# Storing 16 of the last 24 output tiles in smaller pieces: RMSNorm and matmul on one core

## The chip, the cores and the metric

One core of a Trainium2 chip runs the kernel. The metric is the device time of one execution in microseconds (us), the median of several runs; lower is better. Profiles show a span, from the first to the last instruction, which is some 1.5 to 2 us shorter than the device time of the same kernel. All times inside a run are counted from the start of its span.

Loads and stores are carried out by 16 DMA engines that move data between the chip's memory and the core. A store is *issued* when it is put on the queue; each engine then moves its share and counts up the store's completion semaphore, and the time of that is called the *landing* on this engine. The *backlog* of an engine is what it was given earlier and has not moved yet.

## The reference

```python
batch, seq, dim, out_dim = 16, 1024, 512, 768        # all float32
rms = np.sqrt(np.mean(x ** 2, axis=-1, keepdims=True) + eps)
x_norm = x / rms * gamma
return np.matmul(x_norm, weight).astype(np.float32)
```

The 16,384 rows are cut into 128 tiles of 128 rows. A tile of output is 128 x 768 float32, 384 KB, or 3 KB on each of 128 partitions. In all 35.13 MB are read and 50.33 MB written.

## The kernel before

TensorE transposes the rows and multiplies in bfloat16; ScalarE and VectorE take turns in scaling a finished tile out of PSUM, the memory that TensorE writes to, into an output buffer `ot` that holds eight tiles; SyncE issues every load and store on one queue (but for the 2 KB of gamma). `stretches` says which tiles are stored together, and a store is issued when the last tile of its stretch is written:

```python
NT, XG, OG = 128, 16, 8
opening = [1, 1, 1, 1, 2, 2]
last = NT // OG - 1                                   # 15: tiles 120 to 127
o_first, o_size = stretches(OG, {0: opening, 1: [4, 4], last - 1: [4, 4], last: [2, 2, 1, 1, 1, 1]})
...
outp = ctx.enter_context(tc.tile_pool(name="out", bufs=3))
...
def store(i):
    first, n = o_first[i], o_size[i]
    if i == first + n - 1:
        nc.sync.dma_start(out=rows(out, first, n), in_=held(o_tiles, OG, first, n))
...
def finish_tile(i, acc, engine):                      # for each tile, in order
    scale(engine, out_tile(i), acc[:, :O], rstd_of[i])
    store(i)
```

Groups that the table doesn't name go by eight. The very last tile is stored in two parts (columns 0 to 511, then the rest). A packet of a store is one partition's run: 24 KB for eight tiles, 12 for four, 6 for two, 3 for one.

Of the kernel before, what the change touches and what calls it, by code (L numbers as in the profile page):

```python
# [18 lines left out]
def kernel(  # L19
# [18 lines left out]
    XG, OG = 16, 8  # L38
# [7 lines left out]
    def stretches(group, parts):  # L46
        first, size, i = {}, {}, 0
        for g in range(NT // group):
            for n in parts.get(g, [group]):
                for t in range(i, i + n):  # L50
                    first[t], size[t] = i, n
                i += n
        return first, size

    opening = [1, 1, 1, 1, 2, 2]
    last = NT // OG - 1
    x_first, x_size = stretches(XG, {0: opening + [4, 4], 1: [4, 4, 8], 2: [8, 8]})
    o_first, o_size = stretches(OG, {0: opening, 1: [4, 4], last - 1: [4, 4], last: [2, 2, 1, 1, 1, 1]})

    def rows(ap, i, n):  # L60
        if i < XG:
# [287 lines left out]
```

## Time and profile before

| | before |
|---|---|
| median of 3 runs, us | 210.98 (210.57 to 211.02) |
| span of the profiled run, us | 209.0 |
| TensorE busy | 96% |
| DMA data queue, share of 16 engines | 97.0% |
| last matmul ends, us | 203.1 |
| last store lands, us | 207.98 |

The last matmul ends 4.8 us before the last byte has landed. The lines of the page, the stretches at the end and the waits stand in the prediction below, with how they are read.

### The profile page before, as it was taken

How to read it: one execution, taken by the hardware profiler on the slowest of the kernel's cores; microseconds unless marked ns; L12 is line 12 of the kernel's file. 1: busy time of each engine (PE TensorE's matmuls, PEld its weight loads, DVE VectorE, ACT ScalarE, POOL GpSimd, SP SyncE). 2: the span in 40 equal slices, each digit the busy share in tenths (PEclk: the TensorE clock that was granted, in tenths of full speed). 3: DMA queues.
4: the chain of work that ended last, by engine and by line, in shares of the span. 5: the costliest groups of instructions: out<-in, count | busy, mean ns of one | idle time of the engine just before them, and what ended most of it. 6: DMA issues, size and time to landing. Idle time of an engine off the chain costs nothing.

```text
span 209.0 us, 3534 instructions
## 1 busy us (share of the span) xinstructions
PE 201.6 (96%) x1298; PEld 137.9 (66%) x1298; DVE 109.0 (52%) x173; ACT 149.6 (72%) x359; POOL 67.0 (32%) x73
## 2 busy tenths in 40 slices
PE   7999999999999999999999999999999999999980
PEld 2466777666766776667766776667667766677640
DVE  0465654654565465456545644654564465456550
ACT  2689987787778778777877777787777778777640
POOL 1357532306331073213623062310633045230000
PEclk9999999999999999999999999999999999999999
DMA  6999999999999999999999999999999999899994
GB/s 231 392 430 422 408 395 436 424 414 439 431 458 411 412 442 425 447 411 437 428 448 419 423 423 442 433 433 417 428 442 447 405 441 414 381 386 386 383 374 182
DMA packets 7077, 85.69 MB, mean 410 GB/s; under 512 B 786, under 2 KB 916, under 8 KB 3476
## 3 DMA queue, kind: packets, MB, share of 16 engines
q1 hardware_dynamic: 7056, 85.46, 97.0%
q8 instruction: 10, 0.16, 0.3%
q14 instruction: 7, 0.06, 0.1%
q10 hardware_dynamic: 4, 0.00, 0.0%
HBM read 35.13 MB, written 50.33 MB: 409 GB/s over the span
## 4 chain that ended last, share of the span: by engine, by line
PE 91%; ACT 3%; DMA 2%; POOL 1%; DVE 1%; issue 0%; SPq 0%
PE ops L168 77%; PE tp L133 13%; DMA xt<-in_x_dram 2%; ACT jk L98 1%; ACT ot L150 1%; POOL xb L94 1%; ACT rms L102 0%; DVE xT L140 0%; PE ops L227 0%; DVE ot L152 0%; SPq L206 0%; DVE rstd L104 0%
## 5 line engine op out<-in xcount | busy, mean ns | idle before, releaser
L168 PE MATMUL ops<-w_bf,xT 128*128 128x256 bf16 (+1 forms) x1024 | 194.2, 326 | 0.3 <-DVE xT L140 0.3
L168 PEld LDWEIGHTS <-xT 128*128 128x128 bf16 x1024 | 100.0, 98 | 56.4 <-DVE xT L140 1.4
L94 POOL CAST xb<-xt 128x1024 bf16<-128x1024 f32 (+1 forms) x67 | 66.3, 1002 | 118.9 <-PE tp L133 72.9
L150 ACT ACTIVATE ot<-ops,rstd 128x768 f32<-128x768 f32 (+1 forms) x65 | 58.1, 894 | 47.2 <-PE ops L168 47.2
L140 DVE COPY xT<-tp 128x1024 bf16<-128x1024 bf16 (+1 forms) x67 | 44.7, 667 | 83.3 <-PE tp L133 83.0
L98 ACT ACTIVATE jk<-xt 128x512 bf16<-128x512 f32 x128 | 78.7, 619 | 0.7 <-DMA xt<-in_x_dram 0.7
L133 PE MATMUL tp<-ident_f,xb 128*128 128x128 f32 x256 | 68.9, 273 | 0.1
L152 DVE TENSOR_SCALAR ot<-ops,rstd 128x768 f32<-128x768 f32 (+1 forms) x65 | 64.5, 993 | 2.9 <-PE ops L168 2.9
L133 PEld LDWEIGHTS tp<-ident_f,xb 128*128 128x128 f32 x256 | 35.9, 141 | 3.8 <-POOL xb L94 0.7
L98 ACT ACTIVATION_READ_ACCUMULATOR jk<-xt 128x1 f32 x128 | 24.4, 191 | 0.0
L102 ACT ACTIVATE rms<-ssq,eps_sb 128x4 f32<-128x4 f32 (+3 forms) x35 | 10.4, 297 | 1.1
L104 DVE RECIPROCAL rstd<-rms 128x4 f32<-128x4 f32 (+3 forms) x35 | 5.9, 167 | 3.3 <-ACT rms L102 3.3
L227 PE MATMUL ops<-warm 128*128 128x512 bf16 x16 | 6.4, 561 | 1.2 <-DVE eps_sb L220 1.2
L227 PEld LDWEIGHTS <-warm 128*128 128x128 bf16 x16 | 1.9, 131 | 3.9 <-issue 2.5
L150 ACT ACTIVATE w_bf<-w_f,g_sb 128x768 bf16<-128x768 f32 x2 | 1.9, 936 | 3.6 <-DMA w_f<-in_weight_dram 3.6
L201 ACT ACT_TABLE_LOAD x1 | 1.3, 1283 | 1.3 <-PEq L330 1.3
L152 DVE TENSOR_SCALAR w_bf<-w_f,g_sb 128x512 bf16<-128x512 f32 (+2 forms) x3 | 1.4, 485 | 1.1 <-DMA w_f<-in_weight_dram 1.0
L241 DVE COPY g_sb<-tp 128x4 f32<-128x4 f32 x1 | 0.2, 162 | 3.1 <-PE tp L239 3.1
L239 PEld LDWEIGHTS tp<-ident_f,g_row 2*128 2x128 f32 x2 | 0.3, 200 | 0.8 <-issue 0.8
L218 DVE MEMSET warm<- 128x256 uint32 x1 | 0.3, 272 | 0.9 <-PEq L330 0.9
L239 PE MATMUL tp<-ident_f,g_row 2*128 2x2 f32 x2 | 0.4, 264 | 0.0
masks.py:199 POOL TENSOR_SCALAR_AFFINE_SELECT ident_f<-ident_f 128x128 f32<-128x128 f32 x1 | 0.3, 292 | 0.1
(6 smaller groups left out, 0.7 us busy)
## 6 DMA issues: line engine op xcount, KB each, us to landing
out_dram<-ot SPq DMA_DIRECT2D x12, 3072.0 KB, 16.3
xt<-in_x_dram SPq DMA_DIRECT2D x5, 4096.0 KB, 23.0
xt<-in_x_dram SPq DMA_DIRECT2D x3, 2048.0 KB, 19.4
out_dram<-ot SPq DMA_DIRECT2D x4, 1536.0 KB, 11.6
xt<-in_x_dram SPq DMA_DIRECT2D x4, 1024.0 KB, 13.2
out_dram<-ot SPq DMA_DIRECT2D x4, 768.0 KB, 10.4
out_dram<-ot SPq DMA_DIRECT2D x7, 384.0 KB, 11.2
w_f<-in_weight_dram SPq DMA_DIRECT2D x2, 768.0 KB, 5.9
```

The lines of the kernel that those rows point to most:

```text
L94: engine.tensor_copy(out=xb_tiles[i // 2][:, i % 2:i % 2 + n, :], in_=held(x_tiles, XG, i, n))
L98: nc.scalar.activation(out=jk, in_=held(x_tiles, XG, i)[:, 0, :], func=AF.Square, accum_out=ssq)
L102: nc.scalar.activation(out=rms[:, :n], in_=ssq[:, :n], func=AF.Sqrt, scale=1.0 / D, bias=eps_sb)
L104: nc.vector.reciprocal(out=rstd[:, :n], in_=rms[:, :n])
L133: nc.tensor.transpose(out=tp_tiles[j][:, t, h, :], in_=words[:, lo:lo + P], identity=ident_f)
L140: nc.vector.tensor_copy(out=dst[:, t:t + n, :], in_=src[:, t:t + n, :])
L150: nc.scalar.mul(out=dst, in_=src, mul=r)
L152: nc.vector.tensor_single_scalar(out=dst, in_=src, scalar=r, op=mybir.AluOpType.mult)
L168: nc.tensor.matmul(out=acc[:, lo:hi], lhsT=xT_tiles[i // 2][:, i % 2, k // 2, :, k % 2], rhs=w_bf[:, k, lo:hi], start=(k == 0), stop=(k == ...
L201: nc.scalar.preload_act_table(AF.Sqrt)
L227: nc.tensor.matmul(out=spare[:, :WIDE], lhsT=warm[:, :P], rhs=warm, start=True, stop=True)
L239: nc.tensor.transpose(out=gp[:, c, :], in_=g_row[:, :, c], identity=ident_f[:2, :2])
```

## The change

The intent: store tiles 104 to 119 in smaller pieces, so that DMA engines which have run dry get something earlier and less is left at the end.

```diff
-    o_first, o_size = stretches(OG, {0: opening, 1: [4, 4], last - 1: [4, 4], last: [2, 2, 1, 1, 1, 1]})
+    o_first, o_size = stretches(OG, {0: opening, 1: [4, 4], last - 2: [4, 4], last - 1: [2, 2, 2, 2],
+                                 last: [2, 2, 1, 1, 1, 1]})
```

Tiles 104 to 111 go by 4 + 4 instead of 8, tiles 112 to 119 by 2 + 2 + 2 + 2 instead of 4 + 4. The edit is a line longer, so line numbers in later profiles are one higher (165 becomes 166).

## The prediction

> **What bounds the kernel now.** I read the page of the kernel before first: busy time, the forty slices, then the chain that ended last.
>
> ```profile
> PE 201.6 (96%) x1298; PEld 137.9 (66%) x1298; DVE 109.0 (52%) x173; ACT 149.6 (72%) x359; POOL 67.0 (32%) x73
> ...
> DMA  6999999999999999999999999999999999899994
> GB/s 231 392 430 422 408 395 436 424 414 439 431 458 411 412 442 425 447 411 437 428 448 419 423 423 442 433 433 417 428 442 447 405 441 414 381 386 386 383 374 182
> ...
> PE 91%; ACT 3%; DMA 2%; POOL 1%; DVE 1%; issue 0%; SPq 0%
> ```
>
> The reader is to see two nearly full resources. TensorE is busy 96% of 209.0 us and 91% of the chain, but the sixteen DMA engines are at nine tenths too (the page puts the data queue at 97.0% of them). The one 8 in the DMA row is in slice 35, from about 178 to 183 us. The change touches only stores after 174 us, so it can act only through the DMA queue and the end of the run. I therefore cut the last 39 us by hand, with the windows view: columns are the stretch, its length, busy us (and instructions) of PE, PEld, DVE, ACT, POOL, the granted clock, the DMA share and GB/s.
>
> ```profile
> 170.00:179.00 9.00, 9.00 (x61) 6.28 (x60) 4.94 (x7) 6.55 (x17) 5.09 (x5) 1.00 1.01 429
> 179.00:182.00 3.00, 3.00 (x21) 2.13 (x20) 1.70 (x3) 2.38 (x7) 1.04 (x1) 1.00 0.75 320
> 182.00:192.00 10.00, 10.00 (x67) 7.00 (x66) 5.46 (x8) 7.55 (x20) 2.08 (x2) 1.00 0.95 406
> 192.00:194.00 2.00, 2.00 (x16) 1.39 (x15) 1.17 (x3) 1.38 (x4) 0.00 (x0) 1.00 0.59 246
> 194.00:199.00 5.00, 5.00 (x35) 3.36 (x33) 3.15 (x5) 2.74 (x7) 0.00 (x0) 1.00 1.00 415
> 199.00:200.50 1.50, 1.50 (x11) 0.95 (x10) 0.16 (x1) 0.90 (x1) 0.00 (x0) 1.00 0.71 291
> 200.50:206.00 5.50, 2.64 (x17) 1.37 (x14) 1.99 (x3) 1.37 (x2) 0.00 (x0) 1.00 1.00 395
> 206.00:208.00 2.00, 0.00 (x0) 0.00 (x0) 0.00 (x0) 0.00 (x0) 0.00 (x0) 0.99 0.14 51
> ```
>
> TensorE never pauses up to 203 us. The DMA engines as a group starve three times, near 180, 193 and 199.5 us, because no store is ready; that is what the change goes after. After 200.5 they are full again, until 206, and then something small drags on to 208. The waits of the DMA-issuing queue after 160 us name the end:
>
> ```profile
> SPq L165 <- DVE ot L152: 41.6, 8, 11.8
> SPq L344 <- DMA out_dram<-ot: 3.5, 1, 3.5
> ```
>
> The first line says that stores wait for results, not for one another. The second is the end of the program, which waits 3.5 us for a store: the last vector result is written at 203.66 us (in the timeline, started 203.18, 0.48 long), the last store is issued at 203.88 and lands at 207.98, and the span ends 1.0 us later. So the end is set by when the last store lands.
>
> **Which engine drags.** The average over engines hides it. A store's completion semaphore gets sixteen updates in the trace, one per DMA engine, so I read each store by engine:
>
> | store (issued at, us) | first 12 landed by | the four late ones |
> |---|---|---|
> | tiles 96-103 (168.87) | 181.85 | 183.62, 184.56, 184.93, 185.14 |
> | tiles 104-111 (181.00) | 189.66 | 190.88, 191.85, 192.37, 192.52 |
> | tiles 112-115 (187.07) | 193.32 | 194.54, 196.02, 196.34, 196.94 |
> | tiles 116-119 (193.15) | 198.22 | 198.24, 199.66, 200.14, 200.60 |
> | tiles 120-121 (196.19) | 200.08 | 200.12, 201.52, 202.09, 202.44 |
> | tiles 122-123 (199.22) | 202.46 | 202.48, 203.32, 204.03, 204.24 |
> | second part of 127 (203.88) | 206.43 | 206.48, 207.12, 207.81, 207.98 |
>
> Twelve or thirteen engines catch up with the stores at each pause and finish by 206.48. Three never do: from 185 us to the end they go from one store to the next, and end 0.6 to 1.5 us after the rest. Instruction fetches explain much of the lag: the trace has ten of 16 KB, some 0.95 us each on one engine, the last three at 156.96, 176.06 and 194.66 us. The bytes that those three engines have left set the end, not the time at which a store is ready.
>
> **What the Trainium skill says.** "DMA: Bandwidth & Descriptors", section "Queues, rings and completion order": on each engine descriptors are consumed in ring order. The trace agrees: on the late engines, landings of successive stores follow one another by exactly the service time, 1.80 to 1.95 us for 6 KB pieces. Its section "Why a DMA increments its semaphore by 16 and not by 1" says that a DMA runs on up to 16 engines that finish independently and the semaphore counts them; the spread of 183.62 to 185.14 after 181.85 is that. Section "Rules for kernel authors" wants at least 1 MiB per DMA for bandwidth. Here a queue with a backlog hardly shows it: packets of 24, 12 and 6 KB took 921, 468 and 239 ns after 170 us, 26.7, 26.3 and 25.7 bytes per ns. Section "Anatomy of one DMA" puts a fixed 2 us on a DMA of the GpSimd path; back to back these stores from SyncE show no such gap, and the last landing is 0.33 us after the last packet's end.
>
> **The change part by part.**
> 1. Tiles 104 to 111: one store of eight (3072 KB) becomes two of four. The first is issued when tile 107 is out, four tiles earlier: 181.00 - 2 x 3.04 = 174.9 us (a pair of tiles takes 3.04 us in the timeline). It removes most of the pause at 180 us: 3 us at a share of 0.75, so 0.75 us of group time.
> 2. Tiles 112 to 119: two stores of four become four of two, issued at about 184.0, 187.1, 190.1 and 193.15. The pause at 193 (2 us at 0.59, 0.8 us) is broken up and moved: with less backlog, the twelve engines now pause before each later store.
> 3. On the twelve engines the end stays: they already wait at 199.7 to 200.1 for the store of 199.22, and from there the remaining stores and their issue times are untouched. End still 206.4.
> 4. On the three late engines nothing is filled, because nothing was empty. Their bytes are the same in smaller pieces. One engine's share, from landing to landing on the late engines: eight tiles 7.28 us, four tiles 3.66, two tiles 1.84. Tiles 104-111: 2 x 3.66 - 7.28 = +0.04. Tiles 112-119: 4 x 1.84 - 2 x 3.66 = +0.04. Sum +0.08; three more completion writes at 9 ns add 0.03. Together +0.1 us on the path that sets the end.
> 5. SyncE issues three more DMAs at 0.33 us: 1 us, beside 41.6 us in which it waits for results, so hidden. Computation, its buffers and their releases are the same: the buffers of tiles 104 to 119 are not reused after.
>
> So the time goes from 210.98 by +0.1 to **211.1 us**.
>
> **Rivals.** (a) *The pauses are filled and the end comes forward.* For it: the group loses about 2 us in the three pauses (0.75 + 0.8 + 0.4). Were the whole backlog gone, the late engines would end with the others: 207.98 - 206.48 = 1.5 us, giving 209.5, a gain of 0.7%. Against: the three engines had no pauses. The bound on any gain is thus under 2% even if I am wrong. (b) *Small stores cost more than the landings show*, say a fixed 0.3 us each on a backlogged engine: three more stores would add 0.9 us, 211.9. Against: the 3 KB stores near the end follow each other at 0.92 to 0.95 us on the late engines for eight packets of 123 ns, no bubble. (c) *TensorE waits for a buffer that a store holds*: the output pool rotates by three groups, tile 112 needs the store of tiles 88-95 (landed 178.06) and tile 120 that of 96-103 (185.14 against its first write at 193.4). Neither is touched, so nothing. (d) *The late engines are others, or less late, in runs without the profiler*: an instruction fetch that falls elsewhere moves the end by up to its 0.95 us, in both kernels. It widens the range, without a direction.
>
> **Range and chances.** The runs before lie from 210.57 to 211.02. From 211.1 I go down to 210.4, half of (a) or a lucky fetch, and up to 211.7, most of (b). Over 2% is 4.2 us either way: no rival reaches half of it. Faster 0.01, within 2% 0.98, slower 0.01.
>
> **What would show it.** Right: pauses at 180 and 193 us smaller or broken up in the slices, the first twelve landings of the last store still near 206.4, three late engines still going without a pause, last landing 207.9 to 208.2, matmuls ending at the same 203.2 us. Wrong: late landings that close up on the twelve, with a last landing near 206.5 (rival a); successive landings of two-tile stores on late engines over 2 us apart (rival b); a new wait of ACT or DVE for a DMA (rival c).

## The result, and the profile after

The changed kernel took 210.95 us (210.82 to 211.13, 6 runs) beside 210.87 us of the kernel before (210.57 to 211.02, 6 runs). The ratio is 1.0007, with a 95% interval from 0.9994 to 1.0020: the same. Ratios here are the mean time of one kernel's fast runs over the mean of the other's fast runs of the same rounds, so they are not quite the ratio of the medians.

First the page of the changed kernel, the lines that answer to those shown of before.

```profile
PE 199.9 (96%) x1273; PEld 137.7 (66%) x1298; DVE 109.0 (52%) x173; ACT 149.6 (71%) x359; POOL 67.0 (32%) x73
...
DMA  6999999999999999999999999999999999999884
GB/s 219 387 429 423 409 405 431 430 409 448 424 451 416 412 437 430 434 437 421 427 448 424 416 437 432 434 429 409 441 426 434 434 429 418 420 417 395 345 336 171
```

The 8 in slice 35 is a 9 now: the pause near 180 us is gone. But two 8s have come in slices 38 and 39. (25 matmul records fewer are a gap in the record, not in the program: weight loads are 1298 in both.) The windows of the changed kernel, with the columns and, from 179 us on, the stretches that the prediction used, say the same in more detail: the last two columns are the DMA share and GB/s.

```profile
179.00:182.00 3.00, 2.95 (x21) 2.10 (x21) 1.70 (x3) 2.38 (x7) 1.04 (x1) 1.00 0.92 393
182.00:192.00 10.00, 9.95 (x67) 6.98 (x67) 5.39 (x8) 7.55 (x20) 2.08 (x2) 1.00 0.99 419
192.00:194.00 2.00, 2.00 (x15) 1.40 (x14) 1.24 (x3) 1.38 (x4) 0.00 (x0) 1.00 0.84 347
194.00:199.00 5.00, 4.95 (x33) 3.39 (x33) 3.07 (x5) 2.81 (x7) 0.00 (x0) 1.00 0.84 344
199.00:200.50 1.50, 1.50 (x11) 0.93 (x10) 0.23 (x1) 0.90 (x1) 0.00 (x0) 1.00 0.49 201
200.50:206.00 5.50, 2.71 (x18) 1.42 (x15) 1.98 (x3) 1.37 (x2) 0.00 (x0) 1.00 0.99 394
206.00:208.00 2.00, 0.00 (x0) 0.00 (x0) 0.00 (x0) 0.00 (x0) 0.00 (x0) 0.73 0.22 81
```

The share rose from 0.75 to 0.92 at 180 us and from 0.59 to 0.84 at 193, and fell from 1.00 to 0.84 and from 0.71 to 0.49 after 194. Idle time was moved from before to behind, not removed. After 206 us there is more left over than before (0.22 against 0.14). The waits of SyncE's queue after 160 us, in us in total, times, longest:

```profile
SPq L166 <- DVE ot L153: 40.5, 11, 11.8
SPq L345 <- DMA out_dram<-ot: 3.7, 2, 3.5
```

Three more stores wait for results, and the end of the program still waits 3.5 us for the last store. Where that comes from is seen engine by engine. As in the prediction, these are the sixteen updates of each store's completion semaphore, one per DMA engine, in us:

| store of the changed kernel (issued at; some left out) | first 12 landed by | the four late ones |
|---|---|---|
| tiles 96-103 (168.94) | 182.22 | 184.33, 184.46, 185.32, 186.18 |
| tiles 104-107 (175.00) | 185.89 | 188.01, 188.12, 189.12, 189.81 |
| tiles 108-111 (181.08) | 189.53 | 191.66, 191.76, 192.94, 193.44 |
| tiles 112-113 (184.11) | 191.37 | 193.50, 193.62, 194.87, 195.28 |
| tiles 116-117 (190.19) | 195.09 | 197.20, 198.75, 198.76, 198.95 |
| tiles 118-119 (193.22) | 196.93 | 199.06, 200.59, 200.65, 200.78 |
| tiles 122-123 (199.29) | 202.53 | 202.76, 204.24, 204.48, 204.50 |
| second part of 127 (203.95) | 206.53 | 206.57, 208.02, 208.28, 208.30 |

Twelve or thirteen engines end by 206.57, where they ended by 206.48 before. Three end 1.4 to 1.7 us later, and they are late already at 182 to 186 us, when the first store that the change touches has not reached them. The slowest landing of tiles 96-103 is a microsecond later in this trace than in that of before (186.18 against 185.14). The change isn't the cause: the store before it was late already (178.93 against 178.06), and it was issued at 156.78 us, long before the first store that is changed. What is, was not looked into; the second trace of the changed kernel has most of it too (185.94).

### The profile page after: what moved, and what is told of

Its sections match the earlier page's. It is cut to its first block, busy times and chain, and to the rows that moved or that the text cites. A ratio compares the mean times of both kernels' runs of the same rounds, so it can differ in the third digit from the quotient of the medians.

```text
span 209.3 us, 3515 instructions
## 1 busy us (share of the span) xinstructions
PE 199.9 (96%) x1273; PEld 137.7 (66%) x1298; DVE 109.0 (52%) x173; ACT 149.6 (71%) x359; POOL 67.0 (32%) x73
## 4 chain that ended last, share of the span: by engine, by line
PE 88%; DMA 3%; ACT 3%; SPq 1%; DVE 1%; issue 1%
PE ops L169 76%; PE tp L134 13%; DMA w_f<-in_weight_dram 3%; ACT jk L99 1%; ACT ot L151 1%; SPq L84 1%; ACT rms L103 0%; DVE xT L141 0%; DVE w_bf L153 0%; DVE ot L153 0%; SPq L207 0%; DVE rstd L105 0%
## 5 line engine op out<-in xcount | busy, mean ns | idle before, releaser
L169 PE MATMUL ops<-w_bf,xT 128*128 128x512 bf16 (+1 forms) x999 | 192.7, 325 | 1.5 <-DVE xT L141 0.3
L228 PE MATMUL ops<-warm 128*128 128x512 bf16 x16 | 5.9, 523 | 1.2 <-DVE eps_sb L221 1.2
```

Source lines behind the costliest of these rows:

```text
L169: nc.tensor.matmul(out=acc[:, lo:hi], lhsT=xT_tiles[i // 2][:, i % 2, k // 2, :, k % 2], rhs=w_bf[:, k, lo:hi], start=(k == 0), stop=(k == ...
L228: nc.tensor.matmul(out=spare[:, :WIDE], lhsT=warm[:, :P], rhs=warm, start=True, stop=True)
```

## The experiments

The theory: once several stores are queued, the end of the run is set by the DMA engines that carry an old backlog (store after store without a pause). For these it only counts how many bytes are left and how much a piece of a given size costs; the time at which a store becomes ready counts only once it is later than the end of their backlog. Rivals: TensorE alone sets the end and stores are hidden; each store costs a fixed amount; the change is worthless whatever the backlog.

### Coarser: both groups by eight

```diff
-... {0: opening, 1: [4, 4], last - 1: [4, 4], last: [2, 2, 1, 1, 1, 1]})
+... {0: opening, 1: [4, 4], last: [2, 2, 1, 1, 1, 1]})
```

> The change reversed: tiles 104 to 111 and 112 to 119 each stored by eight. Theory (the end is set by the DMA engines that carry a backlog, so the hour at which a store is ready only counts once it is later than that backlog's end): the store of tiles 112-119 is issued at 193.15 us, after the late engines have landed the one before (192.5 us in the trace of the kernel before), so now all sixteen engines wait for it. From the issue 1.4 us to the first byte's landing, 7.28 for the eight, 2 x 1.84, 3 x 0.94, 0.64 and 0.34 us make a last landing near 209.3 us, up to 210.2 on an engine that also fetches instructions, where it was 207.98: 212.2 to 213.2 us in all. Rival (TensorE alone sets the end, stores are hidden): 210.9, as before. Rival (fewer and larger stores are cheaper, so coarser is better): under 210.9.

Measured: 212.51 us (212.34 to 212.78) against 210.79 us of before, ratio 1.0080 (1.0067 to 1.0093). The windows of this run around the store of tiles 112-119:

```profile
182.00:192.00 10.00, 10.00 (x67) 7.01 (x66) 5.16 (x8) 7.55 (x18) 2.08 (x2) 1.00 0.80 338
192.00:194.00 2.00, 2.00 (x16) 1.44 (x14) 1.48 (x3) 1.38 (x6) 0.00 (x0) 1.00 0.00 0
194.00:199.00 5.00, 5.00 (x35) 3.36 (x33) 2.84 (x5) 3.04 (x7) 0.00 (x0) 1.00 1.07 457
```

Between 192 and 194 us the share is 0.00: hardly a packet started, even on the late engines, whose last landing of the store before is at 193.04. All sixteen then land tiles 112-119 within 0.2 us of each other (202.0 to 202.22) and end together, at 209.77 to 209.96. The late engines are gone, and the run is longer by 1.7 us (within the range that was expected), because now the readiness of a store (issued at 193.45) binds. So store timing matters, but on one side of a threshold only: by fours, tiles 112-119 were already on the safe side of it. TensorE as the sole bound falls (matmuls ended at 203.4 us here, 0.3 us from before), and so does "larger is cheaper".

### Finer: tiles 104 to 127 one by one

```diff
+... {0: opening, 1: [4, 4], last - 2: [1] * 8, last - 1: [1] * 8, last: [1] * 8})
```

> The change overdone: each of the tiles 104 to 127 stored alone. Theory: the late engines pay only the landing time of the smaller pieces, 0.94 us a tile instead of 7.28 for eight, 3.66 for four and 1.84 for two: +0.24 for tiles 104-111, +0.20 for 112-119, +0.08 for 120-123, together +0.5 us: 211.2 to 211.6. Rival (each store costs a fixed 0.3 us on a backlogged engine): fifteen more stores, +4.5 us, 215. Rival (stores earlier, so the end earlier): under 210.5.

Measured: 211.66 us (211.28 to 211.83), ratio 1.0037 (1.0025 to 1.0049), 0.8 to 0.9 us over before where 0.5 was expected, and just above the range. A fixed 0.3 us per store, 4.5 us in all, falls. On the late engines the landings follow one another mostly by 0.92 to 1.0 us; the slowest ones of tiles 104 to 126 took 0.95 us a tile (185.68 to 207.61) instead of the 0.94 assumed, some 0.3 us in all. The trace is of the fastest of these runs (211.28 us), with the last landing at 208.56. The waits of the issuing queue after 160 us show something else that was not expected:

```profile
SPq L165 <- DVE ot L152: 18.0, 7, 11.8
SPq L165 <- DMA out_dram<-ot: 6.9, 3, 6.0
```

Stores now wait for stores, once for 6.0 us. The store of tile 111 was issued at 185.74, just after tiles 96-103 had landed on the last engine (185.68). That is the eighth DMA before it, and the trace shows both on the same completion semaphore: this build turns over eight semaphores on the queue, and waits before it uses one again. The late engines stayed fed all the same, as the spacing of their landings shows. The changed kernel never has such a wait.

### The backlog taken away, with the stores of before

```diff
-        if i == first + n - 1:
+        if i == first + n - 1 and first != 96:
```

The result is wrong: tiles 96 to 103 are never stored.

> Wrong on purpose: the store of tiles 96-103 is left out, with the stores after it as in the kernel before. It takes 7.3 us of work off every DMA engine at 169 us, so that the late engines catch up before tile 104's store is ready; computation is the same. Theory: the last landing moves from 208.0 to about 206.9 us (206.4 as on the engines without a backlog, plus what one instruction fetch at 194 us still costs, as there is one short pause after it): 209.7 to 210.2 us in all. Rival (the last stores' own latency or TensorE sets the end): 210.9, as before.

Measured: 209.78 us (209.64 to 209.87), ratio 0.9948 (0.9936 to 0.9960). Fifteen engines land the last store by 206.48 and one at 207.02, with 206.4 and 206.9 expected. The matmuls ended at 203.1 us, exactly as before. The wait at the end is a microsecond shorter than the 3.5 us of before:

```profile
SPq L344 <- DMA out_dram<-ot: 2.5, 1, 2.5
```

The one late engine first shows up in the store of tiles 116-119 (199.57 where fifteen have 198.23), behind an instruction fetch of 16 KB at 193.59 us. The record of the fetch lasts 0.95 us, but the engine is 1.34 us behind. It halves its lag only in the pause at 199.5 us (0.8 us behind in the next stores). So computation was the same, and a microsecond went with the backlog.

### The backlog taken away, with the stores of the changed kernel

The same edit in the changed kernel, wrong in the same way.

> Wrong on purpose: as the run before it, with the stores of tiles 104 to 119 by fours and twos as in the changed kernel. Theory: without the old backlog the change can pay, because each engine has a pause of about a microsecond before the stores at 196 and 199 us, in which the engine with the fetch catches up as well: last landing about 206.5 us, 209.3 to 209.7 in all, 0.2 to 0.6 us under the run before it. Rival (the change is worthless whatever the backlog): the same as the run before it.

Measured: 209.23 us (209.03 to 209.89, 6 runs), ratio 0.9928 (0.9914 to 0.9942), a little under the range that was expected. All sixteen engines land the last store between 206.14 and 206.32. Windows of this run, then its wait at the end:

```profile
194.00:199.00 5.00, 5.00 (x34) 3.40 (x33) 3.30 (x5) 2.55 (x7) 0.00 (x0) 1.00 0.74 296
199.00:200.50 1.50, 1.50 (x11) 0.87 (x9) 0.11 (x1) 0.90 (x1) 0.00 (x0) 1.00 0.47 197
```

```profile
SPq L345 <- DMA out_dram<-ot: 2.1, 1, 2.1
```

There is idle time on every engine now (0.74 and 0.47), and the engine that lost time to the fetch (193.87 where the others have 193.17, and 1.33 us behind in the next store) has caught up two stores later. The wait at the end is 2.1 us, where it is 3.5 in both full kernels. The change is worth about 0.5 us here: 209.78 - 209.23 by the medians, 0.4 us by the ratios. That is not all of it the change's for certain: these six runs spread by 0.9 us, and in the trace the matmuls ended 0.2 us earlier than in the run before it (203.0 us), a shift that is there from 12 us on. What doesn't depend on the shift is the lag: one engine ended 0.5 us behind the others there, none does here. So filling the pauses does bring the end forward where no backlog is left; in the full kernel the backlog hides it.

### What makes an engine late: more instructions to fetch

In the changed kernel, 128 empty instructions of SyncE follow each of eight stores:

```diff
             nc.sync.dma_start(out=rows(out, first, n), in_=held(o_tiles, OG, first, n))
+            if 40 <= first < 104:
+                for _ in range(128):
+                    nc.sync.drain()
```

> What makes engines late? The changed kernel, with 128 empty drain instructions of SyncE after each of the eight stores of tiles 40 to 103: 1024 more instructions of 64 bytes, 64 KB more to fetch through the DMA engines, next to no work otherwise. Theory (an instruction fetch holds up one engine by 0.31 us for 8 KB or 0.95 us for 16 KB, and in a queue that never runs dry this is never made up): instruction packets grow from 0.22 to about 0.29 MB, the lags of single engines grow, and the end comes later by as much as falls on the engines that are latest: 0 to 3 us, most likely about 1 us, 211.5 to 212.5. Rival (late engines are slow for another reason, fetches don't matter): the lags of the last store stay between 1.4 and 2.0 us and the time within 0.2 us of 210.95.

Measured: 217.32 us (217.00 to 218.36), ratio 1.0307 (1.0282 to 1.0333). The direction was right and the size wrong: 6.5 us, not 0 to 3. From the page, a DMA queue (packets, MB, share), then windows, then waits of the issuing queue after 160 us:

```profile
q14 instruction: 15, 0.12, 0.1%
```

```profile
170.00:175.00 5.00, 4.99 (x33) 3.24 (x31) 2.25 (x5) 3.02 (x6) 0.00 (x0) 1.00 1.02 439
175.00:180.00 5.00, 2.89 (x19) 2.11 (x21) 1.46 (x4) 3.01 (x8) 4.04 (x5) 1.00 0.96 412
```

```profile
SPq L348 <- DMA out_dram<-ot: 6.6, 2, 6.3
```

Eight instruction packets of 8 KB came on top of seven. From 120 us on one engine fell further and further behind the median of the sixteen, from 3 to 10 us. The last load of x had landed on fifteen engines by 169.64 us and on that one at 175.82. TensorE had to wait for it (2.89 us busy out of 5), and the last matmul ended at 206.6 us instead of 203.2; then the last store landed at 214.49 on that engine and by 209.90 on the others. In each of these stores one landing stands alone behind the others, so it is taken to be one engine; the trace doesn't number them. Both halves of the loss, some 3.3 us in the computation and 2.8 us more of lag at the end (4.6 us instead of 1.8), then trace back to it. Three reservations. The extra instructions also delayed the issue of the last loads, by some 5 us; but these landed on the twelve fast engines at 167.47, beside 167.7 in the changed kernel, so the delay is not what counted. And 64 KB cost one engine 7 us, while a recorded packet of 8 KB takes 0.31 us; what holds the engine for the rest of the time isn't shown. Nor did any run execute as many instructions without fetching them, so that the fetches are the cause is likely, not shown.

### One part alone

```diff
+... {0: opening, 1: [4, 4], last - 2: [4, 4], last - 1: [4, 4], last: [2, 2, 1, 1, 1, 1]})
```

> One part alone: tiles 104-111 by fours, tiles 112-119 by fours as before. Theory: the late engines pay 2 x 3.66 - 7.28 = 0.04 us, nothing else counts: 210.8 to 211.0, same as the kernel before. Rival (the two parts of the change work against each other, a gain in one and a loss in the other): this one leaves 210.9 by more than 0.3 us.

Measured: 211.14 us (211.00 to 211.64), ratio 1.0009 (0.9988 to 1.0030): the same, though 0.1 us above the range that was expected.

```diff
+... {0: opening, 1: [4, 4], last - 1: [2, 2, 2, 2], last: [2, 2, 1, 1, 1, 1]})
```

> The other part alone: tiles 104-111 by eight as before, tiles 112-119 by twos. Theory: the late engines pay 4 x 1.84 - 2 x 3.66 = 0.04 us: 210.8 to 211.0, same as the kernel before. Rival (the parts cancel each other): away from 210.9 by more than 0.3 us, to the other side than the run before it.

Measured: 211.42 us (211.00 to 211.84), ratio 1.0020 (1.0000 to 1.0041), on a chip where the kernel before spread from 210.63 to 211.86. The median is 0.4 us above the expected range, and the interval is at the edge, so this part and the whole change were run again side by side on another occasion.

> The changed kernel once more, beside the run after it on one chip, to see how far 0.2% can be trusted. Theory (a tenth of a microsecond from landing to landing): ratio to the kernel before 1.000 to 1.001, as in the first measurement (1.0007).

> Twos for tiles 112-119 alone, once more; the first time its ratio was 1.0020 with an interval from 1.0000 to 1.0041, on a chip where the kernel before spread up to 211.86 us. Theory (0.04 us): the same as the run before it within 0.2 us, ratio 0.999 to 1.001. Rival (twos cost more when tiles 104-111 go by eight, because the later stores then queue behind one long one): ratio 1.002 again, 0.3 us or more over the run before it.

Measured: the changed kernel 211.03 us, ratio 1.0007 (0.9994 to 1.0021), once more; the twos alone 210.90 us, ratio 1.0011 (0.9999 to 1.0024). The two are the same within the noise, and the parts don't cancel each other. A cost of one or two tenths of a microsecond in either part can be neither shown nor excluded. In both traces of the twos alone, the matmuls ended 0.5 us later than in the others (203.8 us), long before the change acts: the load of the second tile of x landed at 7.5 us instead of 6.6, the load after it was issued 0.7 us later, and from 12 us to the end TensorE runs 0.6 to 0.7 us behind the trace of before. Why that load is later in both was not looked into.

No version came up that beats the kernel before and stays correct. The run with the changed stores and without the backlog shows what there would be to win: about 1.5 us, or 0.7%.

## Why the prediction was right

The time alone tells little here: all the forecast's rivals would have come out as "the same" too, so it's the landings and the runs without the backlog that carry the account.

- **Bound**: right. The matmuls end at 203.2 us in both kernels, and the end waits for a store. Taking away DMA work alone, with the same computation, moved the time by 1.0 us.
- **Step 1 and step 2** (the pauses): right. The pause at 180 us shrank (0.75 to 0.92) and that at 193 us broke up and came back before the later stores (0.84 and 0.49).
- **Step 3** (the twelve engines end where they did): right, 206.53 against 206.43. What binds them is the readiness of the last stores, which is untouched.
- **Step 4** (the late engines pay 0.08 us for the smaller pieces): fits, as far as the traces can tell. They don't number the engines, but landings can be matched from store to store by the length of their steps. One late engine that meets no instruction fetch in this stretch then lands at 185.14, 192.37, 196.02 and 199.66 us before, 14.52 us for tiles 104 to 119, and goes from 186.18 to 200.78 after, 14.60 us: +0.08 (14.59 us in the second trace of the changed kernel). With one trace of before this is a check, not a proof, and in time the interval is wider than the effect: 210.95 us measured, 211.1 forecast from a median of 210.98 that became 210.87 with three more runs. The slowest landings can't be compared as they stand: before, the one at 200.60 belongs by the same matching to the engine that met the fetch at 194.66 us (191.85 to 196.94 for four tiles, 5.09 us instead of 3.66).
- **Step 5** (three more issues are hidden): right; the queue waits for results as before, and never for another store.
- **Rival (a)**, a gain of up to 1.5 us from filled pauses: rejected here. Where the backlog is gone, the end does come forward by some 1.5 us, to 209.23 us with the changed stores: 1.0 us by the missing backlog and about 0.5 us by the change.
- **Rival (b)**, a fixed 0.3 us per store: rejected by the one-by-one run, which lost 0.8 us over fifteen more stores.
- **Rival (c)**, TensorE waiting for a buffer that a store holds: no such wait in the trace after 150 us.
- **Rival (d)**, the latest engines differ from run to run: open. The slowest landing of tiles 96-103 differed by 1.0 us between the traces of before and after, but by 0.24 us between the two traces of the changed kernel (186.18 and 185.94), and no run without the profiler shows its engines.
- That fetches explain much of the lag was argued in the prediction, with a fetch of 16 KB taken at the 0.95 us of its record. The size was too small: in the two runs without the backlog, where one engine alone is late, it is 1.34 and 1.33 us behind. That the three late engines of the original kernel owe all of their lag to fetches is not shown. One engine is 1.5 us behind the median at 8 us already, and the first fetch of the span comes at 21.62 us. And one of the three, matched as in step 4, takes some 5% longer for the same store than the other two (7.59 us for eight tiles, 3.82 and 3.80 for four, where they need 7.23 to 7.29 and 3.64 to 3.66).

## What to carry to other kernels

An average DMA share with pauses in it does not mean that filling the pauses helps: look at the sixteen landings of a store, and ask whether the engines that land last had a pause at all. Splitting stores pays as long as their readiness binds (by eight it cost 1.7 us here), and stops paying at the point where the slowest engine's backlog is longer than the wait. To see which side a kernel is on, leave a store out and look at the end.

## What the Trainium skill lacked or had wrong

- "Runtime: NRT & Kernel Launch", section "Instruction fetch mechanics", says that the cost of crossing a 16 KiB boundary is "mostly hidden". TensorE shows no pause at the fetch of 194.66 us (5.00 us busy out of 5.00 from 194 to 199 us), but the DMA engine that carries it does lose time: a fetch of 16 KB is recorded with about 0.95 us and left one DMA engine 1.34 and 1.33 us behind the others. With 64 KB of added instructions one engine fell from 3 to 10 us behind, and the run took 6.5 us longer (ratio 1.0307). The page doesn't say that a fetch falls on a single DMA engine.
- "DMA: Bandwidth & Descriptors", section "Rules for kernel authors", asks for at least 1 MiB per DMA. In a queue with a backlog, stores of 3072, 1536 and 768 KB cost the late engines 7.28, 3.66 and 1.84 us, the same per byte within 1.1%; stores of 384 KB cost 0.94 us, 3% more. The rule didn't bind here.
- No page says how to find late DMA engines from the landings of a store; it would belong to "Perfetto Trace Analysis". They show in the spread of the sixteen landings of one store: 0.2 us where all engines have had a pause (202.0 to 202.22 with eights), 5.4 us (179.78 to 185.14) where they have not.
